# A two-layer hybrid backbone: two buffers for RWKV's blocks, the modulation computed beside the projection and the MLP, three banks and row groups for RWKV's preparation

## Chip, cores and metric

The kernel runs on one core of a Trainium2 chip. The metric is the device time of one execution in microseconds (us), the median of several. Engines are named as in the profile: PE (TensorE matmul), PEld (its weight loads), DVE (VectorE), ACT (ScalarE), POOL (GpSimd), SP (SyncE, which here only issues transfers).

## What is computed

Two layers over 256 context tokens and 1024 latent tokens, 1024 columns wide, all in float32. Each layer is modulated by a vector that depends on the condition alone, not on the tokens:

```python
mod = silu(c) @ ada_w[i] + ada_b[i]          # 1024 -> 6 * 1024: shift, scale, gate for each half
h   = rmsnorm(x, norm1_g) * (1 + scale1) + shift1
z   = h @ w_in[i]                            # one projection, its columns shared by four head groups
y   = concat(s5(z), rwkv7(z), retention(z), gla(z))     # each scans forward and backward, summed
x   = x + gate1 * (y @ w_out[i])
h   = rmsnorm(x, norm2_g) * (1 + scale2) + shift2
x   = x + gate2 * (square(relu(h @ mlp_w1[i])) @ mlp_w2[i])
```

A final RMS norm gives the output. RWKV-7 is a recurrence with a rank-one correction at each token; in chunks of tokens it needs the inverse of unit triangular matrices. Its decay `w` and gate `a` come from a 32-column piece of `z` each, by small matrices `w_up` and `a_up`.

## The kernel before

Activations are kept with features on the partitions. A large product is three matmuls per tile (`mm3`): each float32 weight, loaded into a raw buffer `w_raw`, is split by `split` into two rounded parts (`w_hi` on ACT, `w_lo` on DVE or POOL), and likewise the activations. The program is written as generators, one per piece of work; `merged` interleaves them by their share of TensorE's estimated time, and a scheduler then fixes one order of instructions on each engine. Each engine, SP's queue of transfers included, works through its own order strictly.

A layer has these stages, with PSUM's eight banks shared out anew in each (`k.psum`):

1. Norm 1; in layer 0 its `x` comes from DRAM.
2. The input projection (`proj`) beside S5 (`s5_all`). Banks: three for `s`, five for `b`. Weights pass through two raw buffers.
3. The head stage: RWKV (`Rwkv.run`), retention and then gated linear attention (`ret_run`, `gla_run`), and three (layer 0) or two (layer 1) thirds of the modulation (`ada`). Banks: two for `u1` (RWKV's first part), two for `u2`, one for `ch`, one for `fi` (the modulation and RWKV's last transposes), two for `b`.
4. Output projection and norm 2.
5. The MLP, 16 slices of 256 hidden columns, with three raw buffers and eight banks.

`ada(i, q)` computes a third of layer `i`'s modulation: 16 tiles of weights `ada_w` of 128 x 1024, each used by two matmuls whose stationary operand has only two columns (the two conditions), written to one of four groups of 32 partitions. Thirds (0,1), (0,2) and (1,0) run in layer 0's head stage, (1,1) and (1,2) in layer 1's; (0,0) runs alone at the start.

RWKV works on ten pairs of units; a unit is 128 tokens in one direction. For each pair:

- `unit1` loads `rw_zin`, makes decay and gate by matmuls of `rw_up` and `rw_zin` (four per unit, with all 128 rows although only 32 of them are not zero), transposes, and computes the scores (matmuls of `rw_ar` and `rw_bk`) into `rw_TE` and `rw_TO`.
- `inv` inverts the pair's 32 x 32 blocks: SP stores them to DRAM (`rw_S<-rw_TE`, `rw_S<-rw_TO`), loads them spread over the partitions (`rw_B<-rw_S`), loads a starting value from DRAM (`rw_Yv<-in_consts`), then POOL makes 31 steps of two operations, lines 527 and 528; here this is called a pass. Four transfers store the result (`rw_S<-rw_Yv`), four load it in place (`rw_DT<-rw_S`).
- `unit2` and `chain` use the inverse (matmuls of `rw_R` and `rw_DT`) and carry the state.

`rw_B` has one buffer (line 517), so a pass's blocks can be loaded only after the last step of the pass before.

## Time and profile before

| | us |
|---|---|
| median of 3 runs | 3921.67 (3921.33 to 3924.95) |
| span of the profiled execution | 3930.7 |
| projection and norm 1, layer 0 (38 to 464) | 426 |
| head stage, layer 0 (464 to 1052) | 588 |
| MLP, layer 0 (1150 to 2072) | 922 |
| projection, layer 1 (2140 to 2503) | 363 |
| head stage, layer 1 (2503 to 3063) | 560 |

The profile lists no other time of the profiled execution than its span, which is 9.0 us above the median. Stages are told apart by what runs in them; their limits are rounded. A busy PE is one with a matmul in flight. "PEclk" is the share of full speed (2.4 GHz) that TensorE was granted.

### The profile page before, as it was taken

To read this page: it belongs to the slowest core of one execution; us is meant where nothing else is said; L and a number is where in the kernel's file an instruction comes from. 1 tells how busy PE (TensorE), PEld (TensorE's weight loads), DVE (VectorE), ACT (ScalarE), POOL (GpSimd) and SP (SyncE) were. 2 spreads that over 40 slices of the span, in tenths; PEclk is the share of its full clock that TensorE was granted. 3 is DMA by queue.
4 is the path that set the end of the run, shared out by engine and by line. 5 is a ranking of instruction groups with operands and counts; after the bars stand their busy time and mean duration, and the time that the engine had idled before them with its cause. 6 is when DMAs were issued, how large, how long until landed. Compare 5 with 4: busy or idle time off the path is not lost.

```text
span 3930.7 us, 61448 instructions
## 1 busy us (share of the span) xinstructions
PE 3589.8 (91%) x23136; PEld 2973.0 (76%) x23136; DVE 2222.0 (57%) x4654; ACT 1475.3 (38%) x2980; POOL 1353.2 (34%) x2690
## 2 busy tenths in 40 slices
PE   6999888888799999999998999788888799999997
PEld 2998766577687888888886987667677678888885
DVE  5875456667555444444448875555667464444445
ACT  4266345755433111111214365346655332111222
POOL 1541256567431111111111451266676321111112
PEclk8999988787799999999999999898778899999998
DMA  5434575532521111111103434663423411111111
GB/s 184 149 111 145 163 210 141 168 92 61 163 89 33 33 44 33 43 33 44 33 27 120 146 115 144 180 177 112 111 73 96 141 54 49 49 43 43 49 53 43
DMA packets 369241, 372.84 MB, mean 95 GB/s; under 512 B 97360, under 2 KB 313104, under 8 KB 368688
## 3 DMA queue, kind: packets, MB, share of 16 engines
q1 hardware_dynamic: 333600, 343.08, 28.8%
q10 hardware_dynamic: 35344, 25.83, 2.1%
q8 instruction: 183, 3.00, 0.3%
q14 instruction: 114, 0.93, 0.1%
HBM read 285.18 MB, written 83.63 MB: 94 GB/s over the span
## 4 chain that ended last, share of the span: by engine, by line
PE 64%; POOL 9%; DMA 9%; DVE 8%; ACT 5%; issue 3%; SPq 1%; ACTq 0%; DVEq 0%; POOLq 0%
PE psb L161 56%; PE psu L161 5%; POOL rw_Yv L528 3%; POOL rw_tmp L527 3%; DMA rw_B<-rw_S 2%; DMA rw_S<-rw_Yv 1%; PE pss L161 1%; PE psfi L161 1%; DMA ada_w<-in_ada_w_dram 1%; DVE s_W L1158 1%; PE psch L161 1%; DVE n_h L1579 1%; DMA gl_v<-z_gvg 1%; DVE w_lo L1478 1%; DVE zm L223 1%
## 5 line engine op out<-in xcount | busy, mean ns | idle before, releaser
L161 PE MATMUL psb<-hh,w_hi 128*128 128x512 f32 (+1 forms) x1784 | 664.6, 374 | 12.9 <-ACT hh L1951 4.5
L161 PE MATMUL psb<-hl,w_hi 128*128 128x512 f32 (+1 forms) x1784 | 662.5, 372 | 6.5 <-DVE hl L1581 6.5
L161 PE MATMUL psb<-hh,w_lo 128*128 128x512 f32 (+1 forms) x1784 | 659.5, 371 | 0.0
L161 PE MATMUL psb<-mh,w_hi 128*128 128x512 f32 (+1 forms) x1600 | 601.2, 377 | 20.1 <-ACT w_hi L1475 15.3
L161 PE MATMUL psb<-mh,w_lo 128*128 128x512 f32 (+1 forms) x1600 | 598.3, 375 | 6.6 <-DVE w_lo L1478 6.6
L161 PE MATMUL psb<-ml,w_hi 128*128 128x512 f32 (+1 forms) x1600 | 600.5, 375 | 0.0
L1932 DVE SCALAR_TENSOR_TENSOR x<-psb,mod,x 128x512 f32<-128x512 f32 (+1 forms) x640 | 436.9, 694 | 273.8 <-PE psb L161 273.0
L1478 POOL TENSOR_TENSOR w_lo<-w_raw,w_hi 128x1024 fp32r<-128x1024 f32 x84 | 215.0, 2560 | 765.2 <-ACT w_hi L1475 574.8
L1950 DVE TENSOR_TENSOR hr<-hr 128x512 f32<-128x512 f32 x160 | 150.5, 941 | 513.6 <-ACT hr L1949 513.5
L1949 ACT ACTIVATE hr<-psb 128x512 f32<-128x512 f32 x160 | 88.7, 555 | 862.7 <-PE psb L161 861.8
L161 PEld LDWEIGHTS psb<-hh,w_hi 128*128 128x128 f32 x1784 | 338.6, 190 | 77.7 <-issue 6.0
L161 PEld LDWEIGHTS psb<-hl,w_hi 128*128 128x128 f32 x1784 | 338.0, 190 | 72.7 <-DVE hl L1581 11.0
L161 PEld LDWEIGHTS psb<-hh,w_lo 128*128 128x128 f32 x1784 | 337.5, 189 | 61.2 <-issue 1.4
L1952 POOL TENSOR_TENSOR hl<-hr,hh 128x512 fp32r<-128x512 f32 (+1 forms) x80 | 95.3, 1191 | 795.0 <-ACT hh L1951 502.9
L161 PEld LDWEIGHTS psb<-mh,w_hi 128*128 128x128 f32 x1600 | 303.7, 190 | 81.1 <-ACT w_hi L1475 17.4
L161 PEld LDWEIGHTS psb<-mh,w_lo 128*128 128x128 f32 x1600 | 303.3, 190 | 67.9 <-DVE w_lo L1478 8.2
L161 PEld LDWEIGHTS psb<-ml,w_hi 128*128 128x128 f32 x1600 | 303.4, 190 | 60.3 <-issue 2.9
L1475 ACT CAST w_hi<-w_raw 128x1024 fp32r<-128x1024 f32 (+1 forms) x208 | 212.8, 1042 | 317.8 <-PE psb L161 268.5
L527 POOL TENSOR_TENSOR rw_tmp<-rw_Yv,rw_B 128x60 f32<-128x60 f32 (+24 forms) x620 | 206.1, 332 | 198.6 <-DMA rw_B<-rw_S 100.0
L161 PE MATMUL psb<-w_hi,hh 128*128 128x256 f32 (+1 forms) x928 | 266.0, 290 | 4.8 <-ACT w_hi L1475 4.7
L161 PE MATMUL psb<-w_lo,hh 128*128 128x256 f32 (+1 forms) x928 | 266.9, 288 | 0.6 <-DVE w_lo L1478 0.6
L161 PE MATMUL psb<-w_hi,hl 128*128 128x256 f32 (+1 forms) x928 | 266.2, 288 | 0.0
(469 smaller groups left out, 6710.2 us busy)
## 6 DMA issues: line engine op xcount, KB each, us to landing
w_raw<-in_mlp_w_dram SPq DMA_DIRECT2D x128, 512.0 KB, 3.6
ada_w<-in_ada_w_dram SPq DMA_DIRECT2D x96, 512.0 KB, 4.4
w_raw<-in_w_in_dram SPq DMA_DIRECT2D x40, 512.0 KB, 5.6
w_raw<-in_w_out_dram SPq DMA_DIRECT2D x32, 512.0 KB, 5.2
rw_zin<-z_rw SPq DMA_DIRECT2D x20, 576.0 KB, 5.9
rw_B<-rw_S SPq DMA_DIRECT2D x20, 512.0 KB
z_rw<-zm SPq DMA_DIRECT2D x14, 640.0 KB, 3.1
x<-in_xT_dram SPq DMA_DIRECT2D x4, 2048.0 KB
```

The source lines that it names most:

```text
L161: return self.t.matmul(out, lhsT, rhs, **kw)
L223: nc.vector.scalar_tensor_tensor(dst[p0:p1], src[p0:p1], mu[p0:p1, j:j + 1], dst[p0:p1], op0=OP.mult, op1=OP.add)
L527: eng.tensor_tensor(o, bc(Yv[:, 0:m, s:s + 1], [128, m, n]), bc(B[:, s:s + 1, s + 1:32], [128, m, n]), op=OP.mult)
L528: eng.tensor_tensor(Yv[:, 0:m, s + 1:32], Yv[:, 0:m, s + 1:32], o, op=OP.add)
L1158: T_ = lambda o, a, b, op: V.tensor_tensor(o, a, b, op=op)
L1475: nc.scalar.copy(hi[:, :n], raw[:, :n])
L1478: e.tensor_tensor(lo[:, :n], raw[:, :n], hi[:, :n].bitcast(F32), op=OP.subtract)
L1579: nc.vector.scalar_tensor_tensor(h, x[:, kt], g[:, kt, cond:cond + 1], r[:, :n], op0=OP.mult, op1=OP.mult)
L1932: V.scalar_tensor_tensor(self.x[b][:, dt_], ps[:, :n], mod[:, 40 + dt_, cnd:cnd + 1], self.x[b][:, dt_], op0=OP.mult, op1=OP.add)
L1949: A.activation(r[:, :n], ps[:, :n], AF.Relu)
L1950: V.tensor_tensor(r[:, :n], r[:, :n], r[:, :n], op=OP.mult)
L1952: (G if j else V).tensor_tensor(hl[:, j, :n], r[:, :n], hh[:, j, :n].bitcast(F32), op=OP.subtract)
```

## The change

- `rw_B` gets two buffers. The pass's starting value is kept on the chip (`yi0`) and copied by POOL, where it was loaded from DRAM each time.
- The modulation leaves the head stages. Layer 0's thirds 1 and 2 run beside its projection and S5; all three thirds of layer 1 run beside layer 0's MLP. Their weights pass through the raw buffers `w_raw` of the projection and of the MLP.
- Banks: the projection has two for `s` and one for `fi`; the head stage three for `u1` and none for `fi` (RWKV's last transposes then take a `b` bank); the MLP seven for `b` and one for `fi`.
- RWKV's decay and gate matmuls use only the 32 rows that are not zero: the decay's rows 0 to 31, the gate's rows 32 to 63, written in turn.

The diff, without comments and docstrings, which go too:

```diff
@@ Rwkv.setup
-        k.consts(w, ("rwm", "rwb", "rst64", "bo2"))
+        k.consts(w, ("rwm", "rwb", "rst64", "bo2", "yi0"))
@@ Rwkv.unit1
-        for o, b, x in ((l1, self.w0h, 0), (ta, self.a0h, 512)):
-            pw = k.ps("u1")
-            for ti in range(2):
-                cs = slice(x + d * 256 + ti * 128, x + d * 256 + ti * 128 + 128)
-                PE.matmul(pw[:, ti * 128:ti * 128 + 128], self.wup[:, cs], lo, start=True, stop=True)
+        pws = [k.ps("u1"), k.ps("u1")]
+        for ti in range(2):
+            for j, pw in enumerate(pws):
+                cs, s = slice(512 * j + d * 256 + ti * 128, 512 * j + d * 256 + ti * 128 + 128), slice(32 * j, 32 * j + 32)
+                PE.matmul(pw[:, ti * 128:ti * 128 + 128], self.wup[s, cs], lo[s], start=True, stop=True)
+        for o, b, pw in ((l1, self.w0h, pws[0]), (ta, self.a0h, pws[1])):
             for ti in range(2):
@@ Rwkv.inv
-        B = w.tile([128, 32, 32], F32, name="rw_B", bufs=1)
+        B = w.tile([128, 32, 32], F32, name="rw_B", bufs=2)
...
-        o, n = _CO["yi0"]
-        nc.sync.dma_start(Yv.rearrange("p i t -> p (i t)"), k.I["consts"][:, o:o + n])
+        eng.tensor_copy(Yv.rearrange("p i t -> p (i t)"), k.c["yi0"])
@@ Net.ada
-    def ada(self, i, q, pool, bufs=2):
+    def ada(self, i, q, pool, bufs=2, raw=False):
+        def buf(name, n, bufs):
+            if raw:
+                return pool.tile([128, self.wsize], F32, name="w_raw", bufs=self.rbufs)[:, 0:n]
+            return pool.tile([128, n], F32, name=name, bufs=bufs)
...
-                    w = pool.tile([128, 1024], F32, name="ada_w", bufs=bufs)
+                    w = buf("ada_w", 1024, bufs)
...
-        r = pool.tile([128, 512], F32, name="ada_r", bufs=1)
+        r = buf("ada_r", 512, 1)
@@ Net.layer
-        k.psum(s=3, b=5)
+        k.psum(s=2, fi=1, b=5)
         self.uready = False
-        merge(k, [(self.proj(i, h, wp, last), 300), (self.s5_all(i, []), 300)])
+        merge(k, [(self.proj(i, h, wp, last), 300), (self.s5_all(i, []), 300)]
+              + [(chain([self.ada(i, q, wp, raw=True) for q in (1, 2)]), 30)] * (not last))
...
-        k.psum(u1=2, u2=2, ch=1, fi=1, b=2)
+        k.psum(u1=3, u2=2, ch=1, b=2)
...
-        ad = [(i, 1), (i, 2)] + ([] if last else [(i + 1, 0)])
-        merge(k, [(chain([self.ada(a, q, w, 2) for a, q in ad]), ADAW * len(ad)), (rw.run(), 165), (chain([self.ret_run(i, last), self.gla_run(i, last)]), 75)])
+        merge(k, [(rw.run(), 165), (chain([self.ret_run(i, last), self.gla_run(i, last)]), 75)])
...
         hid = self.pool(tag + "hid", "left")
+        k.psum(fi=1, b=7)
...
-        run(self.mlp(i, h, hid, ob, after))
+        mlp = [(self.mlp(i, h, hid, ob, after), 800)]
+        if not last:
+            mlp.append((chain([self.ada(i + 1, q, self.wpo, raw=True) for q in range(3)]), 40))
+        merge(k, mlp)
```

The scheduler's order shows the change at three places.

SP's queue, layer 0's head stage, before: the second pair's blocks are loaded (`rw_B`) right ahead of the store of the first pass's result (`rw_S_5313<-rw_Yv`), with stores of the third pair's scores around them.

```order
L514 DMA rw_S<-rw_TE 32x8x32
L518 DMA rw_B<-rw_S 128x1x1024
L531 DMA rw_S_5313<-rw_Yv 256x1x32 x4
L514 DMA rw_S<-rw_TE 32x8x32
L514 DMA rw_S<-rw_TO 32x8x32 x2
```

In the changed kernel the second pair's blocks are loaded directly behind the stores of its own scores:

```order
L515 DMA rw_S<-rw_TE 32x8x32 x2
L515 DMA rw_S<-rw_TO 32x8x32 x2
L519 DMA rw_B<-rw_S 128x1x1024
L1010 DMA rt_v<-z_ret_399 128x256
L374 DMA rw_zin<-z_rw_393 128x11x128
```

Eleven rows further down it is the third pair's load that stands ahead of the first pass's result. So a load now stands one pass ahead of where it stood.

PE, layer 0's head stage, before: `rw_R,rw_DT_4762` are the matmuls that need the inverse of pair 3 (pairs are counted from 0), `rw_ar,rw_bk` the scores of pair 5.

```order
L161 MATMUL psu_7591<-rw_R,rw_DT_4762 128x128 x4
L161 MATMUL psu_7632<-rw_R,rw_DT_4762 128x128 x4
L161 MATMUL psb_7746<-gl_L,gl_AT 128x256
L161 MATMUL psb_7757<-gl_L,gl_AT 128x256
L161 MATMUL psu_7969<-rw_up,rw_zin 128x256
L165 MATMUL psu_8169<-c_ident,rw_ar 128x128 x2
L161 MATMUL psfi_9315<-ada_w,condsl 2x512 x4
L161 MATMUL psu_7784<-rw_tmp_7596,rw_AO_4768 128x128 x4
L161 MATMUL psu_8176<-rw_ar,rw_bk 128x128 x4
L161 MATMUL psu_8177<-rw_ar,rw_bk 128x128 x4
```

In the changed kernel (`psu_8030` holds scores of pair 5, `rw_DT_4918` the inverse of pair 3, `rw_zin,rw_up` is pair 6's decay and gate):

```order
L161 MATMUL psu_8030<-rw_ar,rw_bk 128x128
L165 MATMUL psb_7645<-c_ident,rt_nq 128x128 x2
L165 MATMUL psu_8043<-c_ident,rw_bk 128x128 x4
L161 MATMUL psu_8295<-rw_VT,rw_TE 64x64 x4
L161 MATMUL psu_8295<-rw_VT,rw_TO 64x64 x4
L161 MATMUL psu_8359<-rw_VT,rw_TE 64x64 x4
L161 MATMUL psu_8359<-rw_VT,rw_TO 64x64 x4
L161 MATMUL psu_8586<-rw_zin,rw_up 128x128 x2
L161 MATMUL psu_8587<-rw_zin,rw_up 128x128 x2
L165 MATMUL psu_8596<-c_ident,rw_zin 128x128 x2
L161 MATMUL psu_8669<-rw_zin,rw_up 128x128 x2
L161 MATMUL psu_7582<-rw_R,rw_DT_4918 128x128 x4
```

The scores of pair 5 moved from behind pair 3's inverse to ahead of it. The order also set the decay's two matmuls (`psu_8586`) one behind the other, and then the gate's two, where the code writes them in turn.

PE, layer 0's MLP, before (`hh` is a hidden tile, `mh` a tile of normalized tokens):

```order
L161 MATMUL psb_13902<-hh,w_lo 128x512
L161 MATMUL psb_13912<-mh_12261,w_hi 128x256
```

In the changed kernel, at the same seam of two groups of 48 matmuls:

```order
L161 MATMUL psb_13868<-hh,w_lo 128x512
L161 MATMUL psfi_13311<-w_raw,condsl 2x512 x2
L161 MATMUL psb_13882<-mh_12186,w_hi 128x256
```

Modulation matmuls now stand at 45 such seams of layer 0's MLP (two matmuls at 43 of them, four at one, six at one) and at 30 places of its projection (two at 28, four at two).

## Rows read from the trace of the kernel before

**Rows 1.** The page, chain of work that ended last by line, shares of the span.
```profile
PE psb L161 56%; PE psu L161 5%; POOL rw_Yv L528 3%; POOL rw_tmp L527 3%; DMA rw_B<-rw_S 2%; DMA rw_S<-rw_Yv 1%; PE pss L161 1%; PE psfi L161 1%; DMA ada_w<-in_ada_w_dram 1%; DVE s_W L1158 1%; PE psch L161 1%; DVE n_h L1579 1%; DMA gl_v<-z_gvg 1%; DVE w_lo L1478 1%; DVE zm L223 1%
```
**Rows 2.** Stages: length, busy us (count) of PE, PEld, DVE, ACT, POOL; PEclk, DMA, GB/s.
```profile
0.00:38.00 38.00, 19.45 (x68) 1.95 (x68) 3.95 (x6) 6.94 (x9) 0.76 (x6) 0.91 0.93 334
38.00:464.00 426.00, 394.91 (x2570) 349.99 (x2570) 289.16 (x759) 209.30 (x346) 135.48 (x264) 0.97 0.40 124
464.00:1052.00 588.00, 490.15 (x4974) 391.64 (x4974) 384.75 (x1030) 320.80 (x863) 368.85 (x999) 0.81 0.49 142
1150.00:2072.00 922.00, 914.77 (x4664) 773.17 (x4663) 432.12 (x612) 188.23 (x289) 139.62 (x89) 0.99 0.12 37
2503.00:3063.00 560.00, 454.46 (x4426) 371.95 (x4426) 356.74 (x938) 297.23 (x803) 344.34 (x946) 0.80 0.44 125
```
**Rows 3.** Tile rw_B: loads in each head stage (ns, first and last start); POOL's idle before a pass.
```profile
L518 SPq DMA_DIRECT2D rw_B<-rw_S x10: 550/568/690, 500.1 to 954.4; - x10
L518 SPq DMA_DIRECT2D rw_B<-rw_S x10: 552/568/585, 2533.0 to 2981.0; - x10
  DMA rw_B<-rw_S: 100.0, 14
```
**Rows 4.** Timeline of SP and POOL at one seam of passes: start, us, engine, what.
```profile
565.59 0.89 SPq L514 DMA_DIRECT2D rw_S<-rw_TO  x2
602.85 0.57 SPq L518 DMA_DIRECT2D rw_B<-rw_S  x1
602.90 0.21 POOL L528 TENSOR_TENSOR rw_Yv<-rw_Yv,rw_tmp 128x8 f32<-128x8 f32 x1
613.97 0.24 POOL L527 TENSOR_TENSOR rw_tmp<-rw_Yv,rw_B 128x31 f32<-128x31 f32 x1 [6.63 <-DMA rw_B<-rw_S]
```
**Rows 5.** Waits on the inverse, layer 0's head stage, then layer 1's: us, times, longest.
```profile
PE psu L161 <- DMA rw_DT<-rw_S: 22.7, 5, 7.6
...
PE psu L161 <- DMA rw_DT<-rw_S: 31.1, 6, 10.6
```
**Rows 6.** Pieces of the chain ahead of the two first passes: start, us, what.
```profile
502.05 11.86 DMA ada_w<-in_ada_w_dram
2533.03 15.56 DMA rw_B<-rw_S
```
**Rows 7.** PE's timeline: modulation matmuls (two records each) and what follows them.
```profile
583.32 1.04 PE L161 MATMUL psfi<-ada_w,condsl 128*2 128x512 f32 x8
584.29 0.44 PE L165 MATMUL psb<-c_ident,rt_nq 128*128 128x128 f32 x2
588.41 1.03 PE L161 MATMUL psfi<-ada_w,condsl 128*2 128x512 f32 x4 [0.56 <-DMA ada_w<-in_ada_w_dram]
589.36 0.44 PE L165 MATMUL psu<-c_ident,rw_zin 128*128 128x128 f32 x2
```
**Rows 8.** PE's timeline: decay matmuls behind 128-row work, and behind 64-row work.
```profile
590.53 0.61 PE L161 MATMUL psu<-rw_zin,rw_up 128*128 128x128 f32 x4
532.35 0.71 PE L161 MATMUL psu<-rw_zin,rw_up 128*128 128x128 f32 x4
```
**Rows 9.** Groups on POOL: copies (count, busy us, mean ns, idle before).
```profile
L303 POOL COPY kk<-zm 128x1280 f32<-128x1280 f32 x4 | 5.1, 1280 | 16.3 <-DMA z_rw<-kk 16.3
L345 POOL COPY rw_RH<-c_ident 64x256 f32<-64x256 f32 x8 | 3.2, 398 | 0.2
```
**Rows 10.** The page, loads of projection weights: count, size, us to landing.
```profile
w_raw<-in_w_in_dram SPq DMA_DIRECT2D x40, 512.0 KB, 5.6
```
**Rows 11.** Head stages by halves (columns as in rows 2), and the modulation's PE time in both.
```profile
464.00:704.00 240.00, 194.81 (x1380) 146.69 (x1380) 147.06 (x391) 121.43 (x329) 150.73 (x379) 0.87 0.61 180
704.00:1052.00 348.00, 295.34 (x3594) 244.95 (x3594) 237.70 (x640) 199.36 (x535) 218.12 (x620) 0.76 0.40 115
2503.00:2715.00 212.00, 172.49 (x1187) 127.10 (x1188) 118.52 (x310) 92.52 (x262) 124.62 (x325) 0.88 0.63 180
sum 1148.00, PE 85.93 PEld 7.19; mean PE 42.96 PEld 3.60
```

More of the change, by code (lines that the diff above doesn't have):

```diff
@@ L1448 @@
 BLK = ((0, 256), (256, 768), (768, 1280))
-ADAW = 8
 FG = ((1, 4, 7), (2, 5))
```

## The prediction, made before the changed kernel was run

> **What bounds the kernel now.** I read the chain of waits first, then the busy time by stage, then the timeline at the seams of the stage that is left. The chain that ended last is 56% matmuls into `psb` [rows 1]: the projections and the MLPs, which run TensorE nearly without a gap (914.77 us busy of 922 in layer 0's MLP, 394.91 of 426 in its projection, at clocks of 0.99 and 0.97) [rows 2]. What is added to PE there lengthens the kernel. The two head stages are different. No engine is full: PE 490.15 of 588 us and 454.46 of 560, at clocks of 0.81 and 0.80, POOL 368.85 and 344.34 [rows 2]. What paces them is POOL's ten passes. The loads of `rw_B` start from 500.1 to 954.4 us, and from 2533.0 to 2981.0, so a pair takes 454.3 / 9 = 50.5 us and 448.0 / 9 = 49.8 us [rows 3]. One seam shows what is in that: the scores of the next pair had been handed to SP by 565.59 + 0.89 = 566.5 us, but their load was issued at 602.85, with the last step of the pass before (602.90 + 0.21), and the next pass began at 613.97 [rows 4]. From one pass's end to the next one's start went 613.97 - 603.11 = 10.9 us, in which POOL did some other work and idled 6.63. In all, POOL idled 100.0 us for that load, 14 times [rows 3].
>
> **The change, part by part.**
>
> Second buffer for `rw_B`. A load needs the scores alone and runs beside the pass before it, so the 10.9 us of a seam go, if the scores are there. Whether they are is a matter of PE's order. Before, the scores of pair n+2 stood behind the matmuls that wait for pair n's inverse, and PE did wait there (22.7 us in 5 waits, 31.1 in 6) [rows 5]; in the changed order they stand behind those of pair n-1 instead, for the passes of pairs 1 to 6 in both layers, while pairs 8 and 9 (in layer 1 pair 7 too) keep the old distance. I take six seams a layer at 10.9 us and the last three at nothing: 2 x 6 x 10.9 = 130.8 us saved. Bounds: all 18 seams, 196 us; and the share that the chain gives to this load, 2% of 3930.7 = 79 us. What is late next is the pass itself: POOL's own busy time is 368.85 / 10 = 36.9 us a pair, so 39.6 a pair still fits.
>
> Starting value on POOL. Twenty loads leave SP's queue, where they waited for a `rw_Yv` buffer with the loads of `rw_zin` behind them. POOL gets 20 copies of 128x256. The nearest rows are copies of 128x1280 at 1280 ns and of 64x256 at 398 ns [rows 9]: between 0.26 and 0.40 us each. POOL sets the pace, nothing hides it: 20 x 0.33 = 6.6 us added (5 to 8).
>
> Modulation out of the head stages. It leaves 85.93 us of PE busy time there [rows 11], on an engine that is not full; I count only what stands ahead of the first pass, where nothing else is under way to cover it. In layer 0 a weight tile of the modulation holds PE's queue, with the first pairs' matmuls behind it, for 11.86 us of the chain [rows 6]; I take 10. In layer 1 the first `rw_B` load took 15.56 us [rows 6] beside the modulation's transfers, against 613.97 - 602.85 = 11.1 at the seam; I take 4.5. Together 14.5 us saved (0 to 27.4, and 86 at the very most if PE were the bound throughout).
>
> Modulation into the full stages. Two matmuls at a seam cost PE 589.36 - 588.41 = 0.95 us from their start to the next one's, and four cost 584.29 - 583.32 = 0.97, since each goes to its own 32 columns [rows 7]. I take 0.96 a row. Projection: 30 x 0.96 = 28.8 us. MLP: 44 rows at 0.96 and the row of six at two of them, 44.2 us. Twenty transposes of 0.11 us (584.29, x2 in 0.44 with the latency of one [rows 7]) are 2.2. Clearing, copying out and adding are for POOL, ACT and DVE, all under half busy there, beside matmuls that do not need them. In the projection 426 - 394.91 = 31 us of PE idle time could hide some: the cost is 44 to 75 us, and I take all 75.2. Two 0.5 MB tiles now stand ahead of `x` in SP's queue at the start, and norm 1 waits for `x`: at the 334 GB/s of that stretch [rows 2] 1.05 MB take 3.1 us more.
>
> New waits. A modulation tile holds a raw buffer from its load until PE comes to its matmuls. Behind the load that waits for a buffer, SP's queue holds the next weights, the stores of S5's matrices and of rotated queries and keys. The MLP has three raw buffers and its next weights are needed a slice later: nothing. The projection has two; nothing taken, a rival below.
>
> Row groups. The decay and gate matmuls could run side by side, two and two: at most half of 40 units x 0.89 us (eight records at full clock by rows 8's rate, (0.61 - 0.17) x 2), 18 us. But the order sets the two of one group one behind the other, so I take no gain. Behind 64-row work the same four records took 0.71 us against 0.61 behind 128-row work [rows 8]; so a change of the array's shape costs about 0.1 us, twice a unit 40 x 0.2 = 8 us of PE time. I take nothing, since PE is not full there, with -18 to +8 as bounds. The Trainium skill ("TensorEngine Tiling (Array Packing)", Key Properties) says that changing the tiling mode drains the engine; the 0.1 us agrees, and by that rule alone the row groups would be a loss of the 8 us just given.
>
> Banks. A third `u1` bank, and a `b` bank fewer in each of the other stages, one `s` bank fewer in both projections: no row shows a wait that ends with a bank alone, and I take nothing.
>
> **The sum.** Saved: 130.8 + 14.5 = 145.3. Added: 6.6 + 75.2 + 3.1 = 84.9. Net -60.4 us. The profiled execution's span is 9.0 us above the median of the runs shown; the differences are small shares of both, so I set them against the median: 3921.67 - 60 = 3861 us. The head stages should give back 65 to 75 us each, layer 0's projection and MLP should grow by about 32 and 45.
>
> **The rivals.**
>
> A. *All seams close.* The last pairs' scores come earlier as well, because everything ahead of them does. Then 196 + 14.5 - 84.9 saves 126: 3796 us. For it: POOL is busy only 36.9 of 50.5 us. Against: three pairs keep the old order. Chance 0.15.
>
> B. *The wait moves to the scores.* PE in the second half is busy 295.34 of 348 us [rows 11]; if the scores are what comes last at most seams, only the chain's share of the load goes: 79 + 14.5 - 84.9 is +9 saved, 3913 us, about no change. Chance 0.15.
>
> C. *The clock falls in the first halves.* With the modulation in them they had 0.87 and 0.88, against 0.76 in the second half that has nearly none [rows 11]; but that half also runs other, smaller matmuls, which speaks against. Without the modulation's some 70 us their PE time is 194.81 + 172.49 - 70 = 297 us, and at 0.76 it takes 297 x (0.875 / 0.76 - 1) = 45 us more: 3906 us if all of that counts. The Trainium skill ("TensorE: Matmul & The Clock Gate", Part 1) says that the clock follows how busy PE has been; these rows fit it but do not separate it from the kind of work. Chance 0.08.
>
> D. *Slower: the projection's two raw buffers starve the weights.* One mechanism: a modulation tile sits in a buffer, so a weight load is issued only when it is due and PE waits its landing of 5.6 us [rows 10]. With 24 loads in layer 0's projection that is up to 134 us; it decides from 11 late loads on (61 us), where the gain is gone; all 24 give 3995 us, and two thirds (90 us) 3951. For it: PE has no slack there, and 32 tiles share two buffers with 24 weights. Against: a buffer turns over every 426 x 2 / 56 = 15 us, three landings. Chance 0.12.
>
> That the change does not do what it says shows only in the row groups, which the order has undone in part; it is in the sum.
>
> **How the numbers follow.** The forecast has the remaining 0.50, at 3861, with its own range of 3830 to 3890 from the copies, the projection's slack and the start of the stages. The range reaches from just below A to just above B: 3790 to 3915. It leaves out D (0.12), a little of A and a little of B, under 0.2 in all. About 0.2% (8 us) is what a measurement of this kernel can tell from no change. Faster by more than that: the forecast, A, most of C and a part of B, 0.77. Within it: the most of what B holds, 0.09. Slower: D and the tail of B, 0.14.
>
> **What would show it.** Right: in the head stages `rw_B` is issued soon after its scores and well before the pass ahead of it ends, POOL's idle time for it falls from 100.0 us to under 30, ten loads span about 390 us in place of 454.3, and both stages end 65 to 75 us sooner; layer 0's MLP takes about 967 us at the same clock. Wrong: a head stage that shortens by under 40 us, with POOL idle for `rw_S` or PE for `rw_DT` at the old seams (B); a clock under 0.80 in the first halves (C); PE waiting for `w_hi` or `w_raw` in layer 0's projection, and a stage of over 480 us there (D).

## The result and the profile after

The changed kernel takes 3972.56 us (median of 4 runs, 3970.56 to 3977.95), against 3923.31 for the kernel before beside it: 1.0118 times as long, with a 95% interval of 1.0097 to 1.0138. Forecast were 3861 us, with a range of 3790 to 3915. The profiled execution spans 3970.3 us.

First the stages of the changed kernel (length, busy us of PE, PEld, DVE, ACT, POOL, then PEclk, DMA share, GB/s), in the order projection, head stage and MLP of layer 0, head stage of layer 1:

```profile
38.00:492.00 454.00, 426.40 (x2706) 351.30 (x2706) 290.31 (x760) 213.80 (x355) 123.03 (x269) 0.97 0.50 153
492.00:1072.00 580.00, 480.30 (x4770) 413.95 (x4770) 381.30 (x1025) 310.23 (x849) 361.24 (x1003) 0.72 0.35 98
1162.00:2141.00 979.00, 972.51 (x4879) 777.97 (x4879) 424.22 (x618) 196.85 (x302) 143.08 (x92) 0.99 0.19 60
...
2563.00:3107.00 544.00, 435.01 (x4290) 375.50 (x4290) 348.38 (x935) 296.64 (x799) 344.05 (x952) 0.75 0.35 95
```

Against [rows 2], the projection has grown by 28 us and the MLP by 57, but the head stages have lost only 8 and 16. In layer 0's, PE is busy 480.30 us, hardly less than the 490.15 of before, although some 50 us of modulation have left it: the granted clock fell from 0.81 to 0.72, and with the row groups PE is 16 us longer busy than without them (e4, below).

Most seams did close. The loads of `rw_B` and POOL's idle time for them (layer 0, layer 1, both), and one seam on POOL:

```profile
L519 SPq DMA_DIRECT2D rw_B<-rw_S x10: 539/560/681, 524.7 to 910.4; - x10
L519 SPq DMA_DIRECT2D rw_B<-rw_S x10: 560/562/580, 2591.4 to 3000.9; - x10
  DMA rw_B<-rw_S: 52.1, 7
```
```profile
621.33 0.21 POOL L528 TENSOR_TENSOR rw_Yv<-rw_Yv,rw_tmp 128x8 f32<-128x8 f32 x1
621.62 0.24 POOL L527 TENSOR_TENSOR rw_tmp<-rw_Yv,rw_B 128x31 f32<-128x31 f32 x1
```

Ten loads span 385.7 us where they took 454.3 [rows 3], at the seam shown the next pass starts 0.08 us after the last step of the one before instead of 10.9 [rows 4], and POOL's idle time for the loads is 52.1 us instead of 100.0. In layer 0 seven of the nine seams are at 0.1 us and those ahead of pairs 8 and 9 stay open (4.6 and 7.2 us); in layer 1 six are at 1.1 us or less and those ahead of pairs 7, 8 and 9 stay open (19.7, 13.4, 7.3): the pairs for which the prediction saw the old order. From the first pass's first step to the last one's end layer 0 takes 414.5 us (497.3 before) and layer 1 443.1 (471.8). That is 112 us; the stages, by the table below, kept 25 of them.

Where it stopped is seen in the last outputs. These rows are the copies of gated attention's outputs (`gl_mix`) and RWKV's (`rw_mix`) in layer 0, with first and last start. Kernel before:

```profile
L1713 ACT COPY gl_mix<-psb x10: 352/372/373, 832.4 to 1029.5; 128x256 f32<-128x256 f32 x10
L1713 ACT COPY rw_mix<-psfi x10: 355/372/394, 703.0 to 1049.0; 128x256 f32<-128x256 f32 x10
```

Changed kernel:

```profile
L1722 ACT COPY gl_mix<-psb x10: 353/372/373, 850.7 to 1039.9; 128x256 f32<-128x256 f32 x10
L1722 ACT COPY rw_mix<-psb x10: 364/373/381, 680.3 to 1067.3; 128x256 f32<-128x256 f32 x10
```

A head stage has two branches, RWKV, and retention followed by gated attention. Before, gated attention ended only 1049.0 - 1029.5 = 19.5 us ahead of RWKV (in layer 1 33). The prediction does not use that row. In the changed kernel the last pass ends at 951.4, and RWKV's last output still comes at 1067.3.

### The profile page after: what moved, and what is told of

Read it like the earlier page. It is cut to its first block, busy times and chain, and to the rows that moved or that the text cites. A ratio compares the mean times of both kernels' runs of the same rounds, so it can differ in the third digit from the quotient of the medians.

```text
span 3970.3 us, 61459 instructions
## 1 busy us (share of the span) xinstructions
PE 3635.5 (92%) x23136; PEld 2998.2 (76%) x23136; DVE 2203.7 (56%) x4654; ACT 1475.3 (37%) x2982; POOL 1336.8 (34%) x2710
## 5 line engine op out<-in xcount | busy, mean ns | idle before, releaser
L1959 DVE TENSOR_TENSOR hr<-hr 128x512 f32<-128x512 f32 x160 | 135.9, 850 | 533.2 <-ACT hr L1958 533.1
L527 POOL TENSOR_TENSOR rw_tmp<-rw_Yv,rw_B 128x60 f32<-128x60 f32 (+24 forms) x620 | 195.8, 316 | 92.8 <-DMA rw_B<-rw_S 52.1
```

Source lines behind the costliest of these rows:

```text
L527: eng.tensor_tensor(o, bc(Yv[:, 0:m, s:s + 1], [128, m, n]), bc(B[:, s:s + 1, s + 1:32], [128, m, n]), op=OP.mult)
L1959: V.tensor_tensor(r[:, :n], r[:, :n], r[:, :n], op=OP.mult)
```

## Experiments

"Head 0" and "head 1" are the lengths of the head stages, from the first decay matmul to the last `rw_mix` copy; "passes" runs from the first pass's start to the last one's end, "tail" from there to the last `rw_mix` (both for layers 0 / 1). In k4 and in layer 0 of l1 gated attention ends after RWKV, so there the stage is longer than "head": 571.4 and 519.5 us in k4, 592.4 in l1.

| kernel | us | ratio to before | head 0 | head 1 | passes | tail |
|---|---|---|---|---|---|---|
| before | 3923.31 | 1 | 578.2 | 549.7 | 497 / 472 | 39 / 39 |
| changed | 3972.56 | 1.0118 | 568.2 | 535.0 | 415 / 443 | 116 / 59 |
| e1 changed, old banks | 4027.77 | 1.0263 | 602.8 | 550.0 | 499 / 477 | 58 / 36 |
| e2 before, second buffer | 3960.43 | 1.0096 | 612.8 | 543.1 | 533 / 467 | 36 / 36 |
| e3 modulation moved alone | 3997.94 | 1.0186 | 579.0 | 552.0 | 489 / 481 | 45 / 37 |
| e4 changed, no row groups | 3950.31 | 1.0069 | 565.0 | 514.8 | 444 / 426 | 83 / 52 |
| g1 e4, old banks | 4001.57 | 1.0201 | 564.1 | 561.5 | 479 / 487 | 42 / 36 |
| g2 e4, one buffer | 4032.45 | 1.0283 | 602.1 | 556.9 | 500 / 467 | 66 / 58 |
| h1 e4, transposes in `u1` | 3936.46 | 1.0023 | 546.5 | 521.6 | 460 / 433 | 48 / 57 |
| h2 e4, six `rw_Y` | 3985.23 | 1.0156 | 574.8 | 542.2 | 449 / 444 | 86 / 66 |
| k1 h1, merged seams | 3907.89 | 0.9950 | 551.7 | 497.5 | 455 / 417 | 57 / 47 |
| k2 h1, filler | 3994.86 | 1.0152 | 593.8 | 531.2 | 503 / 453 | 46 / 37 |
| k3 e4, 32 rows in turn | 3994.17 | 1.0168 | 581.4 | 543.1 | 441 / 450 | 101 / 60 |
| k4 h1, half passes | 3954.89 | 1.0066 | 497.5 | 481.9 | 399 / 380 | 62 / 70 |
| l1 before, half passes | 3948.98 | 1.0052 | 564.5 | 572.8 | 437 / 483 | 86 / 50 |
| l2 h1, modulation-like filler | 3966.01 | 1.0099 | 564.8 | 529.0 | 469 / 446 | 53 / 42 |
| l3 h1, no gated attention | 3733.51 | 0.9504 | 434.8 | 419.1 | 355 / 344 | 37 / 37 |
| l4 h1, no RWKV | 3485.03 | 0.8871 | - | - | - | - |

The intervals reach at most 0.0028 to either side of the ratio. Differences in the text are of medians where nothing else is said; by the ratios they come out up to 8 us otherwise. One caution holds for all: the scheduler orders every engine anew for each kernel, so a part of a difference can come from that order alone. What is read below as an effect is one that more than one kernel shows or that a row explains; how large the order's own part can be is seen in k1, where a stage that the edit does not touch gets 24 us shorter.

### One part at a time: e1 to e4

e1, which tests whether the bank given away delays the end:

```diff
-        k.psum(u1=3, u2=2, ch=1, b=2)
+        k.psum(u1=2, u2=2, ch=1, fi=1, b=2)
```


> The changed kernel with the head stages' PSUM banks of the kernel before: two for the preparation, one that only the last transposes of RWKV's outputs use, two for the rest. Theory 1 (the end of a head stage is late because those last transposes now wait for a bank that gated attention also uses, and hold the buffers the last pairs' chains need): the first latents' transposes come back to some 470 us after the stage's start instead of 497, the last pairs' chains follow their inverses by about 20 us instead of 65, and the two head stages get 20 to 30 and 10 to 15 us shorter, so 3930 to 3945 us. Theory 2 (TensorE's clock, lower since the modulation no longer fills it, sets the end): the same time within 8 us, 3964 to 3980. Theory 3 (retention and gated attention set the end of the stage whatever RWKV does): the same within 8 us too, but with RWKV's last chains early and gated attention's last outputs where they are.

4027.77 us, 55 slower than the changed kernel: none of the three theories. The tail did shorten (116 to 58 us), but the passes went back to 499. The third `u1` bank, which the prediction counted at nothing, is worth more than the lost `fi` bank costs.

e2:

```diff
-        B = w.tile([128, 32, 32], F32, name="rw_B", bufs=1)
+        B = w.tile([128, 32, 32], F32, name="rw_B", bufs=2)
-        merge(k, [(chain([self.ada(a, q, w, 2) for a, q in ad]), ...
+        merge(k, [(chain([self.ada(a, q, w, 1) for a, q in ad]), ...
```


> The kernel before with only the second buffer for the blocks (and one buffer instead of two for the modulation's weights in the head stages, which makes the room for it). If the passes on POOL set the end of a head stage as the prediction read it, the seams of some 11 us go and the two stages get 55 to 75 us shorter each: 3790 to 3830 us. If the banks and the modulation's move are what held the changed kernel back, the gain is at least 60 us here (3860 or less). If something other than the passes ends the stage (gated attention, or the clock), the stages get under 15 us shorter each and the time is 3895 to 3925.

3960.43, slower. The load no longer waits for the buffer, but for the scores: the loads of layer 0 in e2, and POOL's idle time for loads in both stages,

```profile
L518 SPq DMA_DIRECT2D rw_B<-rw_S x10: 545/560/689, 500.9 to 1005.1; - x10
  DMA rw_B<-rw_S: 103.2, 10
```

span 504.2 us instead of 454.3. In layer 0 each load is issued 1.3 to 3.3 us behind the store of its scores, and the scores of pairs 6 to 9 are handed to SP 27, 33, 47 and 59 us later than before. In e2's order half of pair 3's scores stand on PE behind half of the matmuls with pair 1's inverse and the rest behind all of them (before: three quarters of them ahead); the changed kernel has all of pair 3's ahead of them, and pair 4's ahead of pair 2's.

e2 is no clean test of the second buffer, for its edit also leaves the modulation one weight buffer, and PE waits longer for those weights (layer 0's head stage, kernel before, then e2):

```profile
PE psfi L161 <- DMA ada_w<-in_ada_w_dram: 8.6, 4, 6.5
```
```profile
PE psfi L161 <- DMA ada_w<-in_ada_w_dram: 29.7, 11, 8.6
```

The clean one is g1 against e3, below.

e3 (the changed kernel with one `rw_B` buffer, the constant by transfer, old banks, no row groups):

> The changed kernel with only the modulation moved: one buffer for the blocks, the constant by a transfer, the old banks in the head stages, no row groups. By the prediction's working the move alone adds 75 us in the full stages and gives 14.5 us back: 3984 us. With the modulation's own price in the MLP at 1.2 us a pair instead of 0.96 it is some 3990 to 3995. If the move also lowers the clock in the head stages so that RWKV's passes come later there (theory 2), it is over 4000. If the head stages of the kernel before were held up by the modulation's matmuls themselves, it is under 3960.

3997.94, by the ratio 73 us for the move alone, where the prediction's terms make 75.2 + 3.1 - 14.5 = 64. The two head stages are as long as before to 2.3 us: neither the 14.5 us nor any of the 86 came back.

e4:

```diff
-        pws = [k.ps("u1"), k.ps("u1")]
-        for ti in range(2):
-            for j, pw in enumerate(pws): ...
+        for o, b, x in ((l1, self.w0h, 0), (ta, self.a0h, 512)):
+            pw = k.ps("u1")
+            ...
```


> The changed kernel without the row groups: the preparation's four matmuls in series again, each over the whole 64 rows, with three banks kept. By the prediction's term the groups are worth nothing: the same within 8 us, 3964 to 3980. If two banks taken at once make the preparation wait for a bank (three in all, two of them held from the start of a unit), it is faster, 3940 to 3960. If the groups do shorten the preparation where the end hangs on it, it is slower by up to 18 us, 3980 to 3990.

3950.31: the changed kernel, with the row groups, is 22 us slower, and e1 against g1 says the same with the old banks (26 us).

### Buffer and bank need each other: g1 and g2

g1 is e4 with e1's line on banks, g2 is e4 with `bufs=1` for `rw_B`.

> The changed kernel without the row groups and with the head stages' old banks (two for the preparation), so: modulation moved, second buffer, the constant on POOL. Measured so far: the modulation's move alone 3998 us, the move with the second buffer and the third bank 3950. Theory 1 (the second buffer closes the seams only if the scores come a pair earlier, and that the third preparation bank allows, not the buffer): no better than the move alone, 3990 to 4030, with ten passes spanning 485 us or more in layer 0. Rival (the second buffer closes the seams by itself and the bank is worth nothing): 3940 to 3960, ten passes in under 445 us.

> The changed kernel without the row groups and with one buffer for the blocks again: modulation moved, three preparation banks, the constant on POOL. Theory 1 (buffer and bank each need the other): the seams come back and the time is near that of the move alone, 3985 to 4005 us. Rival (the bank does it alone, since the scores were what was late): 3945 to 3965. If the end of the stage does not depend on the passes at all (theory 3), it is within 8 us of 3950 while the passes span 480 us again.

With e3 and e4 that makes a table of four (e3 alone also loads the constant instead of copying it):

| | two `u1` banks | three `u1` banks, no `fi` |
|---|---|---|
| one buffer | 3998 (e3) | 4032 (g2) |
| two buffers | 4002 (g1) | 3950 (e4) |

The buffer is worth nothing without the bank, and the bank costs 34 us without the buffer; the tails are 21 us longer in each layer (e3 45 / 37, g2 66 / 58). Together they bring 48. g2 is above both of its ranges. Beside the buffer the bank is worth about the same with the row groups (55 us, e1 against the changed kernel) as without them (51, g1 against e4).

### The tail: h1 and h2

In the changed kernel RWKV's last transposes (of `rw_Y`) stand among gated attention's users of the two `b` banks. The line that makes their data ready and the transposes, first and last start; before, changed, h1:

```profile
L628 DVE TENSOR_TENSOR rw_Y<-rw_Y,rw_YQ x8: 406/425/616, 933.9 to 1047.6; 128x256 f32<-128x256 f32 x8
L165 PE MATMUL psfi<-c_ident,rw_Y x16: 272/273/474, 941.1 to 1048.4; 128*128 128x128 f32 x16
```
```profile
L628 DVE TENSOR_TENSOR rw_Y<-rw_Y,rw_YQ x8: 410/425/533, 890.7 to 1066.0; 128x256 f32<-128x256 f32 x8
L165 PE MATMUL psb<-c_ident,rw_Y x16: 272/421/477, 995.8 to 1066.8; 128*128 128x128 f32 x16
```
```profile
L627 DVE TENSOR_TENSOR rw_Y<-rw_Y,rw_YQ x8: 415/425/534, 944.0 to 1044.9; 128x256 f32<-128x256 f32 x8
L165 PE MATMUL psu<-c_ident,rw_Y x16: 272/302/472, 944.9 to 1045.7; 128*128 128x128 f32 x16
```

h1:

```diff
-        po = k.ps("fi")
+        po = k.ps("u1")
```


> The changed kernel without the row groups, with RWKV's last transposes taking one of the three preparation banks instead of one of the two that gated attention uses. In the trace of the changed kernel the first latents' output is ready for its transposes at 891 us and they run at 996; in the kernel before, 934 and 941. Theory 1 (that wait, and the last pairs' chains that stand behind it, is what eats the gain of the passes): the transposes follow their data within 20 us, the time from the last pass's end to the end of the stage falls from 83 us to 40 to 50 in layer 0 and from 52 to some 40 in layer 1, and the time is 3895 to 3920 us. Theory 2 (the clock sets the end) or 3 (gated attention does): the transposes come early but the stages end where they did, 3940 to 3960.

3936.46, 14 us better than e4. The transposes follow their data within 5 us, the first within 1 where they were 105 late, and layer 0's tail falls from 83 to 48 us as expected. But its passes grow by 16, layer 1 gets 7 longer, and the time misses the range by 16 us: half of the gain is given back inside the stage.

h2 (`name="rw_Y", bufs=6`):

> The changed kernel without the row groups and with six buffers instead of three for RWKV's outputs (rw_Y), so that the last pairs' chains no longer need a buffer that a late transpose frees; the transposes keep waiting for their bank. If the held buffers are how the late transposes lengthen the stage, the chains of the last two pairs follow their inverses within 25 us and the stages get 15 to 30 us shorter in layer 0 and some 10 in layer 1: 3910 to 3935 us. If the transposes' own place behind gated attention sets the end, chains are early but the time is 3940 to 3960.

3985.23, slower, and outside both ranges. The second chains of pairs 7 and 8 start earlier (954 and 998 us, in e4 1020 and 1035), the last one does not (1052, 1051), and both stages grow. The buffers held chains up, but not the end.

### What the end hangs on: k4, l1, l3, l4

k4 is h1, and l1 the kernel before, with

```diff
-        for s in range(31):
+        for s in range(15):
```


> The kernel of h1 with 15 of the 31 steps of each pass on POOL (the inverse is then incomplete); a pass's own work falls from some 20 us to about 10. If the passes still set the pace of a head stage, ten of them in each give 60 to 150 us a stage: under 3820. If TensorE, 80 to 87 percent busy in every stretch of the stage, sets it now, each stage gets under 25 us shorter: 3885 to 3930.

> The kernel before with 15 of the 31 steps of each pass on POOL (the inverse is incomplete). The prediction's reading (POOL's ten passes pace a head stage): a pass's own work falls by some 10 us, and with it the stage by 80 us or more in each layer: under 3770. Theory 3 (a head stage ends with the later of two branches, RWKV and retention with gated attention, which share TensorE; gated attention ended only 19 and 33 us before RWKV in the kernel before): at most those 52 us, 3875 or more, and if gated attention gets later as RWKV gets earlier, as in k4, 3905 to 3950.

Both got slower than what they were made from, by 18 and 20 us. POOL's idle time for loads of `rw_B`, and the outputs of layer 0, in l1:

```profile
  DMA rw_B<-rw_S: 158.2, 14
```
```profile
L1713 ACT COPY gl_mix<-psb x10: 352/372/373, 881.7 to 1063.5; 128x256 f32<-128x256 f32 x10
L1713 ACT COPY rw_mix<-psfi x10: 360/373/392, 682.6 to 1035.6; 128x256 f32<-128x256 f32 x10
```

In l1 POOL's steps are busy 201 us in both layers together instead of 419, but the ten passes span 437 and 483 us instead of 497 and 472: most of what POOL saves it idles, 158.2 us of it for the loads, against 100.0 [rows 3]. RWKV ends 13 us earlier, gated attention 34 later, and the stage ends with the later one (in k4 it is 49 earlier and 39 later; in l1's layer 1 both come later). So POOL's work in the passes did not pace the stage, in the kernel before either.

l3 and l4 each leave one branch out:

```diff
-        merge(k, [(rw.run(), 165), (chain([self.ret_run(i, last), self.gla_run(i, last)]), 75)])
+        merge(k, [(rw.run(), 165), (chain([self.ret_run(i, last)]), 25)])                          # l3
+        merge(k, [(chain([self.ret_run(i, last), self.gla_run(i, last)]), 75)])                    # l4
```


> The kernel of h1 with gated attention left out of both head stages (zeros take the place of its output). Theory 3 (the two branches share TensorE, and each alone would end far earlier): RWKV's last output comes 60 us or more earlier than the 546 and 522 us of h1. Rival (RWKV's own chain of passes, inverses and states sets its end): within 25 us of them. Time of the whole: for the first under 3800, for the second 3870 or more.

> The kernel of h1 with RWKV left out of both head stages (zeros take the place of its output), so retention and then gated attention alone. Theory 3: their last output, 533 and 517 us after the start of the stage in h1, comes before 400. Rival (retention and gated attention are a chain of their own that is as long as the stage): after 480.

RWKV's last output in l3, gated attention's in l4, both layer 0:

```profile
L1725 ACT COPY rw_mix<-psu x10: 372/372/379, 687.9 to 936.5; 128x256 f32<-128x256 f32 x10
```
```profile
L1725 ACT COPY gl_mix<-psb x10: 372/373/373, 713.9 to 836.4; 128x256 f32<-128x256 f32 x10
```

In h1 they come at 1047.6 and 1033.9; the stage begins near 500 in all three. RWKV beside retention alone needs 435 us, retention and gated attention alone some 340; together they take 546. Neither branch's own chain is as long as the stage, so what they share sets its end. PE is the fullest of it: in every stretch of 150 us up to 950 it is busy 118 to 129 us in h1 and 122 to 129 before. That it is PE and not the other queues that both branches also use is the likeliest reading, and the kernels that load PE alone speak for it (k2, and the row groups: 30 us more of PE's busy time, 22 us more in all); a kernel that relieves PE alone was not made, so it is not shown.

### The clock, and what PE's time is worth: k2, l2

k2 and l2 put work back into h1's head stages, once as full matmuls, once in the modulation's form:

```diff
                 PE.matmul(pw[:, ti * 128:ti * 128 + 128], self.wup[:, cs], lo, start=True, stop=True)
+                PE.matmul(pw[:, 256:512], self.wup[:, cs], self.wup[:, 0:256], start=True, stop=True)          # k2
+                for j in range(4):                                                                           # l2
+                    PE.matmul(pw[32 * j:32 * j + 2, 256:512], self.wup[:, 0:2],
+                              self.wup[:, 256 * j:256 * j + 256], start=True, stop=True)
```


> The kernel of h1 with 80 more matmuls of 256 columns in each head stage, into the half of the preparation's banks that is not used, with no transfer and no bank of their own; nothing reads what they write. At full clock one takes some 0.43 us, so 34 us of TensorE's time a stage. Theory 2 (the clock fell from 0.89 to 0.77 in the first 150 us of the stage because the modulation no longer fills TensorE, and that ate the gain): the granted clock there rises to 0.84 or more, the other matmuls get shorter, and the stages stay within 10 us: 3930 to 3955 us. Rival (TensorE is all but full there, and work put in lengthens the stage): clock below 0.82 and 25 to 45 us more a stage, 3985 to 4025.

> The kernel of h1 with fillers in the form of the modulation: 80 groups of four matmuls of 256 columns with a stationary operand of two columns, side by side in the four groups of 32 partitions, in each head stage, into the unused half of the preparation's banks, with no transfer; nothing reads them. In TensorE's columns that is 40 groups of the modulation's kind, against 48 and 32 in the kernel before. If the modulation was free in the head stages because its kind of work raises the granted clock (0.89 in the first 150 us, against 0.77 without it), the clock rises to 0.84 or more there, the stages stay within 10 us, and the time is 3925 to 3955. If it was free only because it filled TensorE's waits while the end hung on something else, the clock stays under 0.82 and the time within the same 3925 to 3955. If TensorE has no room, as k2 showed for its kind of filler, each stage gets 25 us longer or more: 3985 or more.

From 500 to 650 and 650 to 800 us (columns as above), in turn before, changed, h1, k2, l2:

```profile
500.00:650.00 150.00, 128.12 (x929) 96.16 (x929) 85.34 (x223) 70.75 (x200) 97.77 (x250) 0.89 0.63 182
```
```profile
500.00:650.00 150.00, 131.52 (x896) 114.70 (x892) 96.57 (x264) 77.04 (x229) 96.94 (x248) 0.76 0.42 113
```
```profile
500.00:650.00 150.00, 128.66 (x896) 115.01 (x897) 99.37 (x272) 74.89 (x225) 95.36 (x236) 0.78 0.44 119
650.00:800.00 150.00, 118.50 (x922) 103.84 (x922) 100.87 (x282) 104.30 (x268) 100.92 (x302) 0.82 0.38 103
```
```profile
500.00:650.00 150.00, 127.15 (x874) 112.06 (x874) 88.77 (x243) 66.37 (x196) 91.12 (x231) 0.80 0.41 115
650.00:800.00 150.00, 136.04 (x958) 119.19 (x955) 98.37 (x265) 107.59 (x261) 99.89 (x288) 0.84 0.38 103
```
```profile
500.00:650.00 150.00, 137.03 (x1142) 103.09 (x1141) 92.35 (x244) 71.34 (x210) 94.20 (x237) 0.87 0.40 115
650.00:800.00 150.00, 129.93 (x1093) 96.13 (x1091) 100.21 (x278) 102.36 (x261) 102.35 (x299) 0.95 0.38 101
```

Full matmuls: the clock hardly moves, and the kernel is 58 us longer (51 by the ratios) for fillers that are busy 107 us on PE. Modulation-like ones: the clock rises to 0.87 and 0.95, and 30 us are added for 124 us of fillers. Those are the sums of l2's two groups, layer 0 and layer 1 (busy us, mean ns of a record | idle before):

```profile
L161 PE MATMUL psu<-rw_up 128*2 128x256 f32 x640 | 63.5, 406 | 0.0
```
```profile
L161 PE MATMUL psu<-rw_up 128*2 128x256 f32 x640 | 60.3, 397 | 0.0
```

The other matmuls ran faster beside them (the scores' 47.0 us of PE time in layer 0 became 41.6): from 500 to 1060 us PE is busy 480.42 us in l2 and 453.45 in h1, 27 more with 63.5 us of fillers. So two of the expected readings are partly right: the clock rises with this kind of work, which pays for much of it, not for all.

### Row groups and seams: k3, k1

k3 is e4 with decay and gate taken from their own 32 rows, one bank at a time:

```diff
+        for j, (o, b) in enumerate(((l1, self.w0h), (ta, self.a0h))):
+            pw, s = k.ps("u1"), slice(32 * j, 32 * j + 32)
+            for ti in range(2):
+                cs = slice(512 * j + d * 256 + ti * 128, 512 * j + d * 256 + ti * 128 + 128)
+                PE.matmul(pw[:, ti * 128:ti * 128 + 128], self.wup[s, cs], lo[s], start=True, stop=True)
```


> The kernel of e4 (no row groups, 3950 us) with decay and gate taken from their 32 rows only, but one bank at a time as before: the row groups' operands without the two banks held together. If it is the change of the array's shape that made the row groups cost 22 us (TensorE's busy time in the two head stages was 16 and 14 us more with them), this costs as much: 3962 to 3980. If it is the two banks held together, it is the same as without them: 3942 to 3958.

3994.17, 44 us slower than e4 and more than expected, so it is not the two banks. What the 32-row matmuls cost is seen at full clock between matmuls of 128 rows, in e4, then in the changed kernel:

```profile
649.67 1.06 PE L161 MATMUL psu<-rw_tmp,rw_AO 128*128 128x128 f32 x8
650.57 0.61 PE L161 MATMUL psu<-rw_zin,rw_up 128*128 128x128 f32 x4
651.01 0.27 PE L165 MATMUL psb<-c_ident,rt_q 128*128 128x128 f32 x1
651.12 0.27 PE L165 MATMUL psb<-c_ident,rt_kb 128*128 128x128 f32 x1
```
```profile
639.58 1.06 PE L161 MATMUL psu<-rw_R,rw_DT 128*128 128x128 f32 x8
640.57 0.71 PE L161 MATMUL psu<-rw_zin,rw_up 32*128 32x128 f32 x4
641.20 0.33 PE L165 MATMUL psb<-c_ident,rt_q 128*128 128x128 f32 x1
641.37 0.27 PE L165 MATMUL psb<-c_ident,rt_kb 128*128 128x128 f32 x1
```

From the start of the eight records ahead to the second record behind go 1.45 us in e4 and 1.79 in the changed kernel: 0.09 more ahead of the four, 0.19 in them and up to the next, 0.06 behind it. The records themselves are not slower: at full clock most take 270 ns, where those of 128 rows take 275, and it is nearly always the first of a run that takes 372. So it is the change of shape on both sides that costs, here 0.34 us for a run of four. The changed kernel has 68 such runs; if each pays this, that is 23 us, most of the 30 by which PE's busy time grew from e4 in the two head stages.

The price of the modulation in the MLP is one seam of the changed kernel:

```profile
1276.54 0.39 PE L161 MATMUL psb<-ml,w_hi 128*128 128x512 f32 x1
1276.77 0.39 PE L161 MATMUL psb<-mh,w_lo 128*128 128x512 f32 x1
1277.09 1.03 PE L161 MATMUL psfi<-w_raw,condsl 128*2 128x512 f32 x4
1278.04 0.39 PE L161 MATMUL psb<-hh,w_hi 128*128 128x256 f32 x1
1278.27 0.28 PE L161 MATMUL psb<-hl,w_hi 128*128 128x256 f32 x1
1278.38 0.28 PE L161 MATMUL psb<-hh,w_lo 128*128 128x256 f32 x1
```

Start to start, a 512-column matmul has 0.23 us and a 256-column one 0.12. Here the first waits 0.09 more before the modulation's and the second is followed 0.11 late. From 1276.77 to 1278.27 go 1.50 us instead of 0.35: the seam costs 1.15, not 0.96. k1, which also gives a version faster than both kernels:

```diff
                     yield
-                    w = buf("ada_w", 1024, bufs)
-                    nc.sync.dma_start(w, ...)            # one tile, two matmuls
+                    ws = {g: buf("ada_w", 1024, bufs) for g in (0, 2)}
+                    ...                                  # both tiles, then four matmuls
```


> The kernel of h1 with the two weight tiles of a row block of the modulation loaded together and their four matmuls written together, so that the order has 32 groups of modulation matmuls in layer 0's MLP instead of 45, and 23 instead of 30 in its projection. If a group costs its two changes of the array's shape and the four matmuls run side by side (1.2 us a group in the MLP by the trace of the changed kernel, 0.9 in the projection, whatever stands in it), 13 x 1.2 + 7 x 0.9 = 22 us go: 3936 - 22 = 3914 us. If the cost goes with the number of matmuls, it is the same within 8 us, 3928 to 3944. If holding two raw buffers at once starves the weights, it is over 3945.

3907.89, 0.9950 of before (0.9933 to 0.9968). The MLP lost 14.5 us against h1 for 13 seams fewer, 1.1 us each. The projection gained nothing (head stage 0 starts 6 us later), and layer 1's head stage is 24 us shorter, which the edit does not explain; it is an order drawn anew. So of the 29 us that k1 gains on h1 only the MLP's 14.5 are the seams'.

## Why the prediction failed

**What bounds the kernel: this step failed.** "What paces them is POOL's ten passes" was read off the seams, POOL's idle time and the waits on the inverse. All of that is in the trace, but it describes a queue that waits, not the one that sets the end. Half passes in the kernel before (l1) should have given 80 us a layer by that reading and gave a loss of 20 in all; in h1 (k4) they lost 18. In its place the runs show a stage that ends with the later of two branches: RWKV without gated attention takes 435 us (l3) and the other branch without RWKV some 340 (l4), where together they take 546. That it is PE which they share is argued, not shown. Two things in the kernel before stood against the step: gated attention's last output only 19.5 us ahead of RWKV's, so that a gain of RWKV's alone could not shorten the stage by more while that output stayed where it was, and PE busy 490.15 of 588 us at a clock of 0.81 [rows 2], which the text called "not full".

**Second buffer, -130.8.** Its mechanism was right: the scores moved ahead, the seams closed where the order said so. Its size did not reach the end: 112 us off the passes (changed against before), and with the bank 48 off the time (e3 to e4). Without the bank nothing (g1) or a loss (e2). The seam that it was read from was also not like the others: there the scores had been with SP for 36 us when their load was issued [rows 4], but for pairs 5 to 9 of layer 0 only 1.4, 5.4, 5.5, 2.9 and 9.5 us (layer 1: 2.6, 19.4, 5.1, 5.0, 3.9). Pair 5's load in the kernel before:

```profile
746.86 0.22 POOL L528 TENSOR_TENSOR rw_Yv<-rw_Yv,rw_tmp 128x8 f32<-128x8 f32 x1
```
```profile
747.38 0.93 SPq L514 DMA_DIRECT2D rw_S<-rw_TO  x2
749.68 0.57 SPq L518 DMA_DIRECT2D rw_B<-rw_S  x1
```

The pass ahead of it ended before the last store of the scores did, so in the second half the scores were nearly as late as the buffer, and a buffer alone could not bring the 10.9 us. The order shown in front of the prediction already held the bank's effect; the text credited it to the buffer.

**Banks, nothing.** Wrong in both directions: the third `u1` bank lets the scores come a pair earlier, the `fi` bank given away makes the last transposes 105 us late (h1 gets 14 us back). That no row shows a wait that ends with a bank alone held, since a bank acts through the order.

**Row groups, nothing, -18 to +8.** 22 us, 26 and 44 in three comparisons (19, 24 and 39 by the ratios), outside the bounds. The change of shape was priced at 0.2 us a unit, 8 us of PE time, and then dropped because PE was held to have room; the rows of e4 and the changed kernel make it 0.34 us a run, some 23 us, and PE's busy time grew by 16 and 14 us in the two stages (e4 to changed). The Trainium skill ("TensorEngine Tiling (Array Packing)", Key Properties) says that a change of tiling mode drains the engine; the runs agree with its sign, and it speaks of these row groups and of the modulation's seams alike.

**Modulation out, -14.5.** Nothing came back (e3). The clock from 500 to 650 us fell from 0.89 to 0.77 there, which is rival C; l2 shows that the modulation's kind of work holds it up.

**Modulation in, +75.2.** The projection was right: the head stage starts 27.7 us later in e3 (28.8 and 3.1 expected); rival D, starved weights, is not seen (PE waits 0.8 us for `w_hi` there). DVE, 289.16 of 426 us busy in the projection [rows 2], was not "under half busy" as the text has it; no run shows that it cost anything. The MLP's term was mis-sized: 44 expected, 52 to 55 measured from norm 2's first sums to the next norm's (the 57 above is between rounded limits), since the seam was counted from the modulation's first start to the next start and missed 0.2 us at its edges. In the kernels with the modulation moved, layer 1's projection ran some 10 us and its MLP 8 to 15 us shorter than in the kernel before; the cause is open.

**Starting value, +6.6.** A copy takes 0.40 us, the upper bound; its share of the time was not measured apart.

By the ratios the move costs 73 us (before to e3), buffer, bank and copy together bring 46 (e3 to e4), and the row groups cost 19 (e4 to changed), 46 in all. That these add up is no test, since they are steps of one chain of kernels. Rival B came nearest in mechanism (the waits did move to the scores, in e2 and g1), but no rival had the two branches in it.

## What to carry to other kernels

Before a gain is credited to the end of a stage, look up when every branch that runs beside it ends, and test the supposed pace by halving it: a queue that idles at its seams may only be waiting for work that is late elsewhere. In a program whose order a scheduler fixes, a buffer and a bank act through the order together, so one of them may be worthless or harmful alone. Small matmuls of another shape cost a change on both sides, so bundle them.

## Not expected of the hardware

The granted clock did not go with PE's busy share: 131.52 of 150 us at 0.76 in the changed kernel (500 to 650 us), 136.04 at 0.84 in k2 and 129.93 at 0.95 in l2 (650 to 800), where matmuls with two stationary columns ran side by side in four groups. The Trainium skill ("TensorE: Matmul & The Clock Gate", Part 1) has the clock follow how busy PE has been; by these rows busy time as the profile counts it does not set it alone. In l4, with RWKV gone,

```profile
650.00:800.00 150.00, 94.83 (x1790) 66.03 (x1788) 99.64 (x285) 75.80 (x184) 56.11 (x164) 0.50 0.25 70
```

PE ran at 0.50, its lower level of 1.2 GHz, for 150 us on end while busy 94.83 of them with gated attention's small matmuls.
